# Routing both token tiles in one set of operations, and w2 in blocks of 256 columns, in a two-layer trunk with experts

## The chip, the cores and the metric

The kernel runs on one core of a Trainium2 chip. The metric is the device time of one launch in microseconds (us); each time is the median of several executions. TensorE (PE) does matmuls, VectorE (DVE), ScalarE (ACT) and GpSimd (POOL) do the elementwise work, and SyncE (SP) issues nearly all loads and stores, in one queue. The weights lie in the core's HBM in float32 and are read once each.

## The reference

A token block of 256 rows by 1024 columns passes through two layers: a state-space mixer (layer 0), then causal attention with forget gates (layer 1). Each is followed by a mixture of 32 experts, of which a token uses two. The part that the change touches is the expert mixer, and of the attention the cumulative sums of the forget gates:

```python
def hier_moe(h, wg, bg, we, be, w1, w3, w2):
    t = h.reshape(-1, d)
    g_logits = (t @ wg + bg).astype(jnp.float32)
    g_prob = jax.nn.softmax(g_logits, axis=-1)
    g_top_v, g_idx = lax.top_k(g_logits, 1)
    p_g = jnp.take_along_axis(g_prob, g_idx, axis=1)
    e_logits = (t @ we + be).astype(jnp.float32).reshape(-1, N_EXPERT_GROUPS, EXPERTS_PER_GROUP)
    e_sel = jnp.take_along_axis(e_logits, g_idx[:, :, None], axis=1)[:, 0]
    top_v, top_i = lax.top_k(e_sel, TOP_K)
    w = jax.nn.softmax(top_v, axis=-1) * p_g
    ...
    for e in range(N_EXPERTS):
        y = (jax.nn.silu(t @ w1[e]) * (t @ w3[e])) @ w2[e]
        out = out + gates[:, e:e + 1] * y.astype(jnp.float32)

# in shared_kv: forget gates, summed over the tokens
    logf = jax.nn.log_sigmoid(fz.astype(jnp.float32) + kv_fb.astype(jnp.float32))
    fcum = jnp.cumsum(logf, axis=1).transpose(0, 2, 1)

# in the trunk, for each layer: h is normalised, shifted and scaled (hn), then
        h = h + gate[:, None, :] * hier_moe(hn, moe_wg[l], moe_bg[l], moe_we[l], moe_be[l],
                                            moe_w1[l], moe_w3[l], moe_w2[l])
```

Here d = 1024, an expert's inner width is 256, there are 4 groups of 8 experts, and TOP_K is 2.

## The kernel before

The 256 tokens lie in two tiles i = 0, 1 of 128 partitions; h[:, i] is a tile's residual stream. All weights come in blocks of 1 MB (128 partitions x 2048 float32) into a ring of slots. `prefetch` and `block` (lines 69 to 84) issue a load on SP's queue as soon as a slot is free; a load waits in the queue until the instructions that read the slot before are done, and everything behind it in SP's queue waits with it. In the expert part of a layer there are 96 such blocks, in the order q = 0 to 7, for each q eight blocks "wa" (w1 and w3 of four experts) and four blocks "wb" (w2 of the same four). In layer 0 more slots are opened once the gated mixer output has been added (line 1052); in layer 1 two more groups of slots were opened in the attention part (lines 1339 and 1442).

One layer's experts, `moe` (line 312): `start` (line 571) has its order on all four compute engines written out by hand. For each tile it adds the second half of the mixer's output to h, turns the rows by four transposes (`across`), takes the sum of squares (`square`, ScalarE) and adds the logits of those columns (`logits`, line 362). Then comes the norm (`norm`, with a power on GpSimd at line 345), four steps of `fill`, which are the matmuls of the output gate (line 188, four blocks of the ring, whose row of biases is loaded by SP behind a GpSimd memset), then the routing. `route_tile` (line 365) is a generator for one tile; the two tiles' generators are run side by side with zip, so VectorE gets each operation twice in turn, 16 pairs from the logits (line 367) to the chosen experts (line 395). `weigh` ranks the tokens of each expert by small matmuls, `place` builds a selection matrix with 32 places for each expert, and `gather` (line 450) multiplies it with h, so that the tokens of four experts stand in 128 columns.

`experts` (line 595) then runs over q. `first` multiplies with the eight wa blocks (line 486): four matmuls for a block, one for each expert, on 32 columns of weights, 512 columns of the block. The activation is turned (line 474, copied at line 476 to aT), and `second` (line 495) multiplies with the wb blocks: block 2n + f holds rows 128 f to 128 f + 127 of w2 of the four experts, columns 512 n to 512 n + 511. Two blocks add up in one PSUM tile of 512 columns, which VectorE multiplies with the output gate into y (line 504). `scatter` (line 508) adds y back to the token rows: one matmul of 512 columns for each tile into four accumulators acc[i][n] that live through the layer. For the last q, `done` is called behind each of these: in layer 0 it adds the accumulator to h (line 259) and takes the sum of squares, in layer 1 it adds and issues the output DMA (line 1468). `overflow` holds a branch for experts with more than 32 tokens.

Where no order is written out, a planner with a timeline of its own orders each engine's instructions. In the attention part TensorE's order is written out, the other engines' is not (line 1145). There `project` (line 1156) runs eight steps of six matmuls (line 1162) and calls `tick` after each step. `tick` advances the first generator in the list `between` by one yield: the norm of the k heads (`head_norm`, lines 1179 to 1188), then `forget_gates` (line 1199), whose last step issues the three small matmuls of lines 1242 to 1244 on the result of a chain of small VectorE operations (lines 1220 to 1239). The accumulators of `project` come from a set of four, two for each call. The weights for each step are split in two parts by ScalarE (line 1104) and VectorE (line 1105), three steps ahead at most.

## Time and profile before

| | before |
|---|---|
| median of 3 runs | 818.82 us (817.67 to 820.29) |
| profiled execution, its own time | 819.66 us |
| its span, first to last instruction | 817.9 us |
| TensorE busy, share of the span | 706.3 us, 86% |
| VectorE busy | 381.3 us, 47% |
| ScalarE busy | 232.1 us, 28% |
| GpSimd busy | 46.7 us, 6% |
| moved by DMA | 299.30 MB, mean 366 GB/s |
| mean granted clock of TensorE | 0.945 |

A row of the timeline gives the start in us, the length in us, the engine, the line of the kernel, the operation, the tiles written and read with their shapes, and how many instructions were merged into the row; in brackets stands the idle time of the engine just before and what released it. PE is the matmul itself, PEld the load of its weights, which overlaps. A float32 matmul leaves two records. PEclk is the granted clock of TensorE as a share of 2.4 GHz.

### The profile page before, as it was taken

What the parts mean: (1) busy time and instruction counts of PE and PEld (TensorE: products, weight loads), DVE (VectorE), ACT (ScalarE), POOL (GpSimd) and SP (SyncE); (2) the same over time, 40 slices, a digit from 0 to 9 for tenths busy, and PEclk for the clock granted to TensorE, in tenths of its full rate; (3) what the DMA queues carried; (4) which work ended last, traced back from release to release, by engine and by line L of the source; (5) the groups of instructions that cost most, each with busy time, mean ns of one, the idle gap of its engine ahead of it and who ended that gap; (6) DMA issues with size and microseconds to landing.
All of it is one profiled execution on the core that took longest, in us unless ns stands there. A gap on an engine that the chain in (4) does not pass through costs nothing. (4 is left out here: it accounts for less than half of the span.)

```text
span 817.9 us, 13668 instructions
## 1 busy us (share of the span) xinstructions
PE 706.3 (86%) x5510; PEld 402.8 (49%) x5510; DVE 381.3 (47%) x1025; ACT 232.1 (28%) x537; POOL 46.7 (6%) x52
## 2 busy tenths in 40 slices
PE   2797999898899998786779899999988999986776
PEld 0674776575533533131157567888764333331311
DVE  7685999774322332111165655775554222221202
ACT  4423333162201110000043265878722101100100
POOL 2000000000000000000001101570000000000000
PEclk9899999998999999789679999999999999999888
DMA  9998946777999999999999857592989999999996
GB/s 368 426 425 347 406 150 250 292 314 277 426 426 426 426 425 425 428 423 427 424 424 426 315 197 312 204 370 98 349 347 415 426 428 424 427 427 427 425 426 260
DMA packets 41828, 299.30 MB, mean 366 GB/s; under 512 B 4632, under 2 KB 4760, under 8 KB 5664
## 3 DMA queue, kind: packets, MB, share of 16 engines
q1 hardware_dynamic: 41344, 297.14, 88.3%
q10 hardware_dynamic: 416, 1.23, 0.4%
q8 instruction: 45, 0.74, 0.3%
q14 instruction: 23, 0.19, 0.1%
HBM read 297.31 MB, written 1.05 MB: 365 GB/s over the span
## 5 line engine op out<-in xcount | busy, mean ns | idle before, releaser
L486 PE MATMUL mm<-w,xg 128*32 128x512 f32 x1024 | 141.4, 637 | 24.0 <-DMA w<-wa 10.7
L486 PEld LDWEIGHTS mm<-w,xg 128*32 128x32 f32 x1024 | 29.6, 111 | 110.6 <-issue 62.8
L458 ACT ACTIVATE xg<-mm,sh,g 128x128 f32<-128x128 f32 x64 | 29.3, 457 | 181.0 <-PE mm L450 164.8
L1105 DVE TENSOR_TENSOR ws<-w,ws 128x512 fp32r<-128x512 f32 x80 | 58.2, 733 | 40.4 <-ACT ws L1104 40.1
L501 PE MATMUL mm<-w,aT 128*32 128x512 f32 x512 | 68.3, 655 | 9.2 <-DMA w<-wb 3.6
L450 PE MATMUL mm<-Pr,h 128*128 128x128 f32 x512 | 65.3, 281 | 11.2 <-DVE Pr L438 11.2
L1162 PE MATMUL acc<-ws,hn 128*128 128x512 f32 x288 | 73.9, 415 | 0.6 <-ACT hn L1140 0.6
L450 PEld LDWEIGHTS mm<-Pr,h 128*128 128x128 f32 x512 | 60.9, 194 | 26.6 <-issue 19.0
L508 PE MATMUL acc<-y,Sc 128*128 128x512 f32 x128 | 64.7, 629 | 6.5 <-DVE y L504 6.5
L1104 ACT ACTIVATE ws<-w 128x512 fp32r<-128x512 f32 x80 | 49.9, 629 | 54.5 <-PE acc L1162 43.6
L1162 PEld LDWEIGHTS acc<-ws,hn 128*128 128x128 f32 x288 | 56.0, 197 | 16.7 <-ACT hn L1140 1.9
L456 DVE TENSOR_SCALAR xg<-mm,g,sh 128x128 f32<-128x128 f32 x64 | 26.2, 410 | 74.1 <-ACT xg L458 74.1
L504 DVE TENSOR_TENSOR y<-mm,gbc 128x512 f32<-128x512 f32 x32 | 22.1, 692 | 64.7 <-PE mm L501 64.5
L491 ACT ACTIVATE a<-mm 128x256 f32<-128x256 f32 x16 | 6.1, 383 | 161.2 <-PE mm L486 161.2
L469 DVE COPY Sc<-mm 128x256 f32<-128x256 f32 x16 | 6.8, 425 | 83.8 <-PE mm L467 83.8
L508 PEld LDWEIGHTS acc<-y,Sc 128*128 128x128 f32 x128 | 22.2, 193 | 45.6 <-issue 26.8
L492 DVE TENSOR_TENSOR a<-a,mm 128x256 f32<-128x256 f32 x16 | 6.7, 419 | 75.0 <-ACT a L491 75.0
L501 PEld LDWEIGHTS mm<-w,aT 128*32 128x32 f32 x512 | 14.4, 114 | 50.6 <-issue 34.4
L785 PE MATMUL mm<-hnT,w 128*64 128x128 f32 x512 | 33.1, 289 | 2.7 <-ACT hnT L255 2.7
L961 PE MATMUL acc<-w,uT 128*128 128x512 f32 x64 | 30.5, 621 | 5.6 <-ACT uT L950 5.5
L785 PEld LDWEIGHTS mm<-hnT,w 128*64 128x64 f32 x512 | 31.3, 143 | 4.4 <-ACT hnT L255 3.7
L173 PE MATMUL mm<-w,sc 128*32 128x256 f32 x512 | 29.2, 380 | 0.0
(327 smaller groups left out, 951.8 us busy)
## 6 DMA issues: line engine op xcount, KB each, us to landing
w<-wa SPq DMA_DIRECT2D x128, 1024.0 KB, 19.5
w<-wb SPq DMA_DIRECT2D x64, 1024.0 KB, 19.7
w<-ada SPq DMA_DIRECT2D x36, 1024.0 KB, 10.6
w<-ada00s SPq DMA_DIRECT2D x8, 1024.0 KB, 18.1
w<-kvada SPq DMA_DIRECT2D x8, 1024.0 KB, 9.0
w<-win SPq DMA_DIRECT2D x4, 1024.0 KB, 14.9
w<-ada00g SPq DMA_DIRECT2D x4, 1024.0 KB, 18.8
w<-woutv SPq DMA_DIRECT2D x4, 1024.0 KB, 17.2
```

What stands on the lines that cost most here:

```text
L173: PE.matmul(ps[32 * q:32 * q + 32, 0:256], sc32(2 * b + kk), bands(w[:, 1024 * kk:1024 * kk + 1024])[:, q], start=b + kk == 0, stop=b == 3 ...
L450: PE.matmul(px[:, 128 * c4:128 * c4 + 128], h[:, i, 128 * c:128 * c + 128], Pr[:, i].rearrange("p a b -> p (a b)"), start=i == 0, stop=i == 1)
L456: V.tensor_scalar(xg[:, c], src, g[:, c:c + 1], sh[:, c:c + 1], op0=OP.mult, op1=OP.add)
L458: S.activation(xg[:, c], src, AF.Identity, bias=sh[:, c:c + 1], scale=g[:, c:c + 1])
L486: PE.matmul(ph[32 * s:32 * s + 32, :], xg[:, k, 32 * s:32 * s + 32], w[:, 512 * s:512 * s + 512], start=k == 0, stop=k == KD - 1)
L501: PE.matmul(py[32 * s:32 * s + 32, :], aT[:, 128 * f + 32 * s:128 * f + 32 * s + 32], w[:, 512 * s:512 * s + 512], start=f == 0, stop=f == 1)
L508: PE.matmul(acc[i][n], scs[q][:, 128 * i:128 * i + 128], y[:, 512 * n:512 * n + 512], start=q == 0, stop=q == NQ - 1, skip_group_check=True)
L785: PE.matmul(ps[64 * v:64 * v + 64, 128 * hh:128 * hh + 128], w[:, k, c0:c0 + 64], hnT[:, k, v::2], start=k == 0 and hh == 0, stop=k == KD ...
L961: PE.matmul(val[t][n], uT[:, m, 128 * t:128 * t + 128], wval[m // 2][:, c0:c0 + 512], start=m == 0, stop=m == 7)
L1104: S.activation(o[:, 0], w, AF.Copy)
L1105: V.tensor_tensor(o[:, 1], w, o[:, 0].bitcast(F32), op=OP.subtract)
L1162: PE.matmul(pk[i], src[:, k, a, 128 * i:128 * i + 128], w[:, b], start=k + a + b == 0, stop=k == KD - 1 and b == 1)
```

## The change

The routing of both tiles becomes one chain: `route` works on tiles of the form [128, 2, w], both token tiles in one instruction, except for the two operations that need a scalar of each tile or more dimensions. The combination of comparing and multiplying in `rank_first` becomes two instructions, since the maximum is now broadcast. That makes 21 instructions in place of 32. In `start` the logits of the second half are issued after both tiles have been turned.

The w2 blocks are laid out anew by the host: block 2n + m now holds all 256 rows of w2 of the four experts for 256 columns, 512 n + 256 m onwards. `second` runs eight matmuls of 256 columns for a block. For the last q, `second_last` multiplies, gates, scatters and adds 256 columns at a time; the output of the last layer is stored in one DMA of 512 columns and two of 256 for each tile, six in all, where four were. In layer 0 the sum of squares is taken behind the second half. The branch in `overflow` is changed to the new layout. In `forget_gates` five empty yields stand ahead of the three small matmuls.

```diff
@@ -362,38 +362,32 @@
                 PE.matmul(pls[0][:, 64 * i:64 * i + 36], hTs[i][:, k, :], sw[:, k],
                           start=k == 0 and i == 0, stop=k == KD - 1, skip_group_check=True)
 
-        def route_tile(pl, i):
-
-            V.scalar_tensor_tensor(lg[:, i], pl[:, 64 * i:64 * i + 36], rstd[:, i:i + 1], c36, op0=OP.mult, op1=OP.add)
-            yield
-            gl = lg[:, i, 0:4]
+        def route(pl):
+
+            for i in range(2):
+                V.scalar_tensor_tensor(lg[:, i], pl[:, 64 * i:64 * i + 36], rstd[:, i:i + 1], c36,
+                                       op0=OP.mult, op1=OP.add)
 
             def rank_first(x, w, mx):
 
-                V.tensor_reduce(mx[:, i], x, axis=AX, op=OP.max)
-                yield
-                V.scalar_tensor_tensor(cand[:, i, 0:w], x, mx[:, i], desc[:, NE - w:], op0=OP.is_equal, op1=OP.mult)
-                yield
-                V.tensor_reduce(top[:, i], cand[:, i, 0:w], axis=AX, op=OP.max)
-                yield
-
-            yield from rank_first(gl, 4, gm)
-            V.tensor_scalar(gc[:, i], cand[:, i, 0:4], top[:, i], -BIG, op0=OP.is_lt, op1=OP.mult)
-            yield
-            V.tensor_tensor(ml[:, i].rearrange("p (a b) -> p a b", b=8),
-                            lg[:, i, 4:36].rearrange("p (a b) -> p a b", b=8),
-                            gc[:, i, :, None].to_broadcast([128, 4, 8]), op=OP.add)
-            yield
-            yield from rank_first(ml[:, i], NE, m1)
-            V.tensor_scalar(o1[:, i], cand[:, i], top[:, i], None, op0=OP.is_equal)
-            yield
-            V.scalar_tensor_tensor(ml2[:, i], o1[:, i], -BIG, ml[:, i], op0=OP.mult, op1=OP.add)
-            yield
-            yield from rank_first(ml2[:, i], NE, m2)
-            V.tensor_scalar(o2[:, i], cand[:, i], top[:, i], None, op0=OP.is_equal)
-            yield
-            V.tensor_tensor(selb[:, i], o1[:, i], o2[:, i], op=OP.add)
-            yield
+                V.tensor_reduce(mx[:, :, 0], x, axis=AX, op=OP.max)
+                V.tensor_tensor(cand[:, :, 0:w], x, mx.to_broadcast([128, 2, w]), op=OP.is_equal)
+                V.tensor_tensor(cand[:, :, 0:w], cand[:, :, 0:w],
+                                desc[:, None, NE - w:].to_broadcast([128, 2, w]), op=OP.mult)
+                V.tensor_reduce(top[:, :, 0], cand[:, :, 0:w], axis=AX, op=OP.max)
+
+            rank_first(lg[:, :, 0:4], 4, gm)
+            V.tensor_tensor(gc, cand[:, :, 0:4], top.to_broadcast([128, 2, 4]), op=OP.is_lt)
+            for i in range(2):
+                V.scalar_tensor_tensor(ml[:, i].rearrange("p (a b) -> p a b", b=8),
+                                       gc[:, i, :, None].to_broadcast([128, 4, 8]), -BIG,
+                                       lg[:, i, 4:36].rearrange("p (a b) -> p a b", b=8), op0=OP.mult, op1=OP.add)
+            rank_first(ml, NE, m1)
+            V.tensor_tensor(o1, cand, top.to_broadcast([128, 2, NE]), op=OP.is_equal)
+            V.scalar_tensor_tensor(ml2, o1, -BIG, ml, op0=OP.mult, op1=OP.add)
+            rank_first(ml2, NE, m2)
+            V.tensor_tensor(o2, cand, top.to_broadcast([128, 2, NE]), op=OP.is_equal)
+            V.tensor_tensor(selb, o1, o2, op=OP.add)
 
         def weigh():
 
@@ -495,20 +489,39 @@
         def second(q, aT, y, n):
 
             py = mm_tile()
-            for f in range(2):
-                w = block("wb", l, q, 2 * n + f)
-                for s in range(4):
-                    PE.matmul(py[32 * s:32 * s + 32, :], aT[:, 128 * f + 32 * s:128 * f + 32 * s + 32],
-                              w[:, 512 * s:512 * s + 512], start=f == 0, stop=f == 1)
+            for m in range(2):
+                w = block("wb", l, q, 2 * n + m)
+                for f in range(2):
+                    for s in range(4):
+                        PE.matmul(py[32 * s:32 * s + 32, 256 * m:256 * m + 256],
+                                  aT[:, 128 * f + 32 * s:128 * f + 32 * s + 32],
+                                  w[:, 512 * s + 256 * f:512 * s + 256 * f + 256],
+                                  start=f == 0, stop=f == 1, skip_group_check=True)
             c = slice(512 * n, 512 * n + 512)
             V.tensor_tensor(y[:, c], py, gbc[:, c], op=OP.mult)
 
-        def scatter(q, y, n, done=None):
+        def second_last(q, aT, y, n, done):
+
+            for m in range(2):
+                py = mm_tile()
+                w = block("wb", l, q, 2 * n + m)
+                for f in range(2):
+                    for s in range(4):
+                        PE.matmul(py[32 * s:32 * s + 32, 0:256],
+                                  aT[:, 128 * f + 32 * s:128 * f + 32 * s + 32],
+                                  w[:, 512 * s + 256 * f:512 * s + 256 * f + 256], start=f == 0, stop=f == 1)
+                c = slice(512 * n + 256 * m, 512 * n + 256 * m + 256)
+                V.tensor_tensor(y[:, c], py[:, 0:256], gbc[:, c], op=OP.mult)
+                for i in range(2):
+                    PE.matmul(acc[i][n][:, 256 * m:256 * m + 256], scs[q][:, 128 * i:128 * i + 128], y[:, c],
+                              start=False, stop=True, skip_group_check=True)
+                    V.tensor_tensor(h[:, i, c], acc[i][n][:, 256 * m:256 * m + 256], h[:, i, c], op=OP.add)
+                    done(i, n, m)
+
+        def scatter(q, y, n):
             for i in range(2):
                 PE.matmul(acc[i][n], scs[q][:, 128 * i:128 * i + 128], y[:, 512 * n:512 * n + 512],
-                          start=q == 0, stop=q == NQ - 1, skip_group_check=True)
-                if done:
-                    done(i, n, acc[i][n])
+                          start=q == 0, stop=False, skip_group_check=True)
 
         def overflow(rv):
 
@@ -556,10 +569,12 @@
                     for n in range(2):
                         w = part("wb", n)
                         py = [mm_tile() for _ in range(2)]
-                        for f in range(2):
-                            for i in range(2):
-                                PE.matmul(py[i], aTs[i][:, 128 * f:128 * f + 128], w[:, f],
-                                          start=f == 0, stop=f == 1)
+                        for m in range(2):
+                            for f in range(2):
+                                for i in range(2):
+                                    PE.matmul(py[i][:, 256 * m:256 * m + 256], aTs[i][:, 128 * f:128 * f + 128],
+                                              w[:, m, 256 * f:256 * f + 256], start=f == 0, stop=f == 1,
+                                              skip_group_check=True)
                         for i in range(2):
                             for c2 in range(2):
                                 r = slice(256 * c2, 256 * c2 + 256)
@@ -578,13 +593,13 @@
                     next(st)
                     across(i, 1)
                     square(ssq, i, 1)
+                for i in range(2):
                     logits(i, 1)
                 after()
                 mb.append(es.enter_context(tc.tile_pool(name=f"moeb{l}", bufs=1, side="right")))
                 norm(ssq)
                 step(fill, 4)
-                for _ in zip(*[route_tile(pls[0], i) for i in range(2)]):
-                    pass
+                route(pls[0])
                 mosti = weigh()
                 place(0)
                 gather(0)
@@ -612,13 +627,12 @@
                     gather(q + 1)
                 aT = turned(a)
                 y = mb[0].tile([128, D], F32, tag="y", name="y", bufs=2)
-                second(q, aT, y, 0)
                 if last:
-                    scatter(q, y, 0, done)
-                second(q, aT, y, 1)
-                if last:
-                    scatter(q, y, 1, done)
+                    second_last(q, aT, y, 0, done)
+                    second_last(q, aT, y, 1, done)
                 else:
+                    second(q, aT, y, 0)
+                    second(q, aT, y, 1)
                     scatter(q, y, 0)
             if l == 0:
                 shrink()
@@ -1055,9 +1069,9 @@
 
     ssq2 = new_ssq()
 
-    def add_square(i, n, src):
-        add(src, i, n)
-        square(ssq2, i, n)
+    def add_square(i, n, m):
+        if m:
+            square(ssq2, i, n)
 
     gb11 = gate_tile(small)
     M.experts(mosti, fill, add_square)
@@ -1238,6 +1252,8 @@
         V.tensor_scalar(fz, fz, 0.0, None, op0=OP.min)
         V.scalar_tensor_tensor(fz, fp, -2.0, fz, op0=OP.mult, op1=OP.add)
         yield
+        for _ in range(5):
+            yield
         pc = mm_tile()
         PE.matmul(pc[:, 0:16], tri, fz[:, 0:16], start=True, stop=True)
         PE.matmul(pc[:, 16:32], ones, fz[:, 0:16], start=True, stop=False)
@@ -1462,10 +1478,10 @@
 
     mosti = M.start(added, ssq, fill, lambda: None)
 
-    def add_out(i, n, src):
-        add(src, i, n)
-        c = slice(512 * n, 512 * n + 512)
-        nc.sync.dma_start(out[0, 128 * i:128 * i + 128, c], h[:, i, c])
+    def add_out(i, n, m):
+        if n or m:
+            c = slice(512 + 256 * m, 768 + 256 * m) if n else slice(0, 512)
+            nc.sync.dma_start(out[0, 128 * i:128 * i + 128, c], h[:, i, c])
 
     M.experts(mosti, fill, add_out)
     er.close()
@@ -1561,7 +1577,7 @@
 
     w13 = np.concatenate([np.asarray(moe_w1), np.asarray(moe_w3)], axis=-1)
     d["wa"] = w13.reshape(2, NQ, 4, KD, 128, 512).transpose(0, 1, 3, 4, 2, 5).reshape(2, NQ, KD, 128, 2048)
-    d["wb"] = (np.asarray(moe_w2).reshape(2, NQ, 4, 2, 128, 2, 512).transpose(0, 1, 5, 3, 4, 2, 6)
+    d["wb"] = (np.asarray(moe_w2).reshape(2, NQ, 4, 2, 128, 4, 256).transpose(0, 1, 5, 4, 2, 3, 6)
                .reshape(2, NQ, 4, 128, 2048))
     return {n: np.ascontiguousarray(a) for n, a in d.items()}
```

## Rows read from the trace of the kernel before

**Rows 1.** Windows: start:end, length, busy us (instructions) by engine, PEclk, DMA share, GB/s.

```profile
200.00:400.00 200.00, 168.50 (x1121) 66.17 (x1113) 47.43 (x150) 20.48 (x45) 0.22 (x2) 0.93 1.01 425
565.00:570.00 5.00, 4.63 (x28) 3.40 (x28) 2.32 (x4) 5.00 (x11) 0.00 (x0) 1.00 0.01 3
...
603.50:606.50 3.00, 3.00 (x32) 1.46 (x34) 2.08 (x17) 0.00 (x0) 1.17 (x2) 1.00 0.01 4
607.00:807.00 200.00, 167.17 (x1117) 65.64 (x1110) 46.76 (x145) 20.48 (x45) 0.00 (x0) 0.94 1.01 424
```

**Rows 2.** Waits of TensorE, 461 to 604 us: releaser, us in total, times, longest.

```profile
PE mm L1242 <- DVE f_z L1239: 3.9, 1, 3.9
PE mm L188 <- DVE xf L1136: 0.9, 1, 0.9
```

**Rows 3.** Windows behind the wait at line 1242, columns as in rows 1.

```profile
462.00:465.00 3.00, 3.00 (x9) 2.32 (x8) 0.17 (x3) 0.63 (x1) 0.00 (x0) 0.50 1.02 430
466.00:470.00 4.00, 4.00 (x19) 3.22 (x18) 1.65 (x3) 1.90 (x3) 0.00 (x0) 1.00 0.02 10
```

**Rows 4.** Timeline of the attention part: head norm of k, and eight steps.

```profile
450.32 0.60 ACT L1179 ACTIVATE sq<-acc 128x512 f32<-128x512 f32 x1 [0.53 <-PE acc L1162]
...
455.92 0.69 DVE L1188 TENSOR_TENSOR kn<-acc,rs 128x512 f32<-128x512 f32 x1
...
489.25 11.45 PE L1162 MATMUL acc<-ws,hn 128*128 128x512 f32 x48
```

**Rows 5.** Timeline of the tail of layer 0.

```profile
403.00 3.78 PE L508 MATMUL acc<-y,Sc 128*128 128x512 f32 x4 [0.80 <-DVE y L504]
...
409.75 1.98 PE L508 MATMUL acc<-y,Sc 128*128 128x512 f32 x4 [0.83 <-DVE y L504]
...
411.77 0.69 DVE L259 TENSOR_TENSOR h<-acc,h 128x512 f32<-128x512 f32 x1 [0.17 <-PE acc L508]
```

**Rows 6.** Timeline: matmuls of 256 and 512 columns, and copies of aT.

```profile
433.20 3.66 PE L173 MATMUL mm<-w,sc 128*32 128x256 f32 x64
...
627.11 0.42 DVE L476 COPY aT<-mm 128x256 f32<-128x256 f32 x1 [0.49 <-PE mm L474]
...
630.13 3.64 PE L501 MATMUL mm<-w,aT 128*32 128x512 f32 x32
...
649.25 0.42 DVE L476 COPY aT<-mm 128x256 f32<-128x256 f32 x1 [0.49 <-PE mm L474]
...
802.97 0.42 DVE L476 COPY aT<-mm 128x256 f32<-128x256 f32 x1 [0.78 <-PE mm L474]
```

**Rows 7.** Timeline of the start of the experts of layer 1.

```profile
596.85 0.60 PE L333 MATMUL mm<-ident,h 128*128 128x128 f32 x4
...
599.21 2.84 PE L362 MATMUL acc<-smallw,hT 128*128 128x36 f32 x24
...
604.31 3.64 PE L188 MATMUL acc<-w,sc 128*32 128x512 f32 x32
...
604.50 0.42 DVE L367 SCALAR_TENSOR_TENSOR lg<-acc,rstds,c 128x36 f32<-128x36 f32 x2 [0.92 <-POOL rstds L345]
...
608.33 0.32 DVE L395 TENSOR_TENSOR selb<-o,o 128x32 bf16<-128x32 f32 x2
...
614.12 7.07 PE L486 MATMUL mm<-w,xg 128*32 128x512 f32 x64
```

**Rows 8.** Timeline of small VectorE operations of 32 and 64 elements.

```profile
459.07 1.32 DVE L1236 SCALAR_TENSOR_TENSOR f_p<-f_p,f 128x32 f32<-128x32 f32 x6
...
608.96 0.23 DVE L410 SCALAR_TENSOR_TENSOR rk<-mm,selb 128x64 f32<-128x64 f32 x1 [0.17 <-PE mm L409]
```

**Rows 9.** Timeline of the tail of layer 1.

```profile
811.06 0.69 DVE L504 TENSOR_TENSOR y<-mm,gbc 128x512 f32<-128x512 f32 x1 [0.34 <-PE mm L501]
...
811.80 1.98 PE L508 MATMUL acc<-y,Sc 128*128 128x512 f32 x4 [0.81 <-DVE y L504]
```

**Rows 10.** Output stores: from the issue to landing, by tile.

```profile
DMA to landing us min/median/max: 2.0/2.0/2.0
```

## The prediction

> **What bounds the kernel now.** First read the load queue over time. From 200 to 400 us, while the experts of layer 0 run, and from 607 to 807 us, while those of layer 1 run, the 16 DMA engines are busy 1.01 of the time at some 425 GB/s [rows 1]. Nothing on the engines can shorten these 400 us; they can only begin or end at another time. Between them lies the attention part, where the DMA engines have free time: between 565 and 570 us they move nearly nothing [rows 1]. There TensorE is the bound. Its list of waits from 461 to 604 us holds one that matters, 3.9 us before line 1242, then 0.9 us [rows 2]. So time can be won at four places: in the tail of layer 0 (from its last blocks to the rows' sums of squares), at line 1242, at the point where the loads of layer 1 start again after a gap (603.5 to 606.5 us, DMA share 0.01 [rows 1]), and in the tail of layer 1, which ends the kernel. What is won ahead of the gap is worth its full length only if the loads ahead of the gap can move forward too; the idle 565 to 570 us say that they wait for free slots there, and slots come free when TensorE and ScalarE have read them.
>
> **Line 1242 (five more yields).** TensorE's order is written out in this part. After two steps of the first v projection it meets the three small products of the forget gates and waits 3.9 us for VectorE's chain of small operations [rows 2]. The wait has a second price: from 462 to 465 us the granted clock is 0.50, that is 1.2 GHz, after TensorE had stood idle, and from 466 us it is 1.00 [rows 3]. 3 us at half speed lose 1.5 us. The new yields let five more steps go first. Eight steps take 11.45 us [rows 4], so five take 7.2 us, against 3.9 us of wait. VectorE must put the splits of weights that feed these steps between the chain; two or three of 0.7 us delay the chain by about 2 us, to some 6 of the 7.2 us. The wait then goes to nothing, and no idle is left to lower the clock: 3.9 + 1.5 = **5.4 us**. The bounds are 3.9 (no gain from the clock) and 5.6 us (half speed until nearly 466). Behind the moved products waits only the first turning of heads, 40 us later. What is moved with them is the head norm of the second half of k, now generated five ticks later; it frees two of the four accumulators that the second v projection wants. In the trace its last multiplication already runs at 455.92 us [rows 4], ten us before that projection, so I cost this at nothing; without that cover it is the first rival.
>
> **Tail of layer 0.** TensorE has idle gaps of 0.80 and 0.83 us where it waits for the gate product of 512 columns on VectorE, and after the second it still has 1.98 us of scatter, then the add of 0.69 us [rows 5]. With blocks by 256 columns a half of y is ready after each block. The first gap closes, for the first half's scatter can begin while the second block is multiplied. In place of the second gap stands the scatter of the half before (half of 1.98). After the last gate product only two matmuls of 256 columns and one add of 256 columns are left. So the last scatter ends 0.80 + 0.83 = 1.63 us earlier and the last add is some 0.27 us shorter (512 columns take 0.69; a 256 column copy from PSUM, line 476, takes 0.42 [rows 6]): **1.9 us**. The work of TensorE stays the same, since 64 records of 128x256 took 3.66 us and 32 of 128x512 took 3.64 us [rows 6]. The low bound is 0.8 us (only one gap closes); the high one is 3.2, if the first scatter, 3.78 us here against 1.98 later [rows 5], runs partly at the higher clock because TensorE has stood idle less before it. Behind this tail TensorE waits for sums of squares and the norm, so the gain passes on whole.
>
> **Start of the experts.** In layer 0 the new order and the new routing change nothing: the loads run at a share of 1.01 throughout [rows 1], and the slack of the ring absorbs either sign. In layer 1 the loads stand still until the ada11 blocks of line 188 are read (from 604.31 us), and a second time they nearly run dry until the first block of line 486 is read (from 614.12 us) [rows 7]. The turned rows of tile 1 now go ahead of all logits of the start. Line 362 takes 2.84 us for 24 records, from 599.21 [rows 7]; with four transposes of 0.6 us ahead of it [rows 7] and eight more records (1.0 us) it ends at 599.2 + 0.6 + 2.84 + 1.0 = 603.65, so line 188 starts 0.66 us earlier and line 367, which then no longer waits for the norm, at 603.75 in place of 604.50 us, 0.75 earlier. Against this stands the routing itself. Now 32 small operations in 16 pairs take 3.83 us from line 367 to line 395 [rows 7], 0.26 a pair: the two tiles' operations overlap, so a pair costs about what one dependent operation costs. After the change there are 21 operations in 19 dependent steps, 18 of them ahead of the last. A dependent step of 32 elements takes 1.32/6 = 0.22 us; 64 elements add about 0.035 (0.225 against 0.19 for one operation) [rows 8]. 0.26 for the logits' pair, 6 x 0.22, 11 x 0.255 make 4.4 us, 0.6 more than now. Line 486 starts 0.75 - 0.6 = **0.15 us** earlier, and this second point decides. Bounds: a loss of 0.7 us (18 steps of 0.30, a pair of now and 64 elements, make 5.3) and a gain of 1.0 (routing much shorter, line 188 deciding). The Trainium skill speaks here for a larger gain (VectorE: DVE Perf Modes, Rules for kernel authors): it tells one to lower the count of chained VectorE operations, since each waits for the pipeline to empty. By that, 21 in place of 32 would take 2.5 us, not 4.4; the trace speaks against it, since independent neighbours here start some 0.13 us apart, closer than their own lengths.
>
> **Tail of layer 1.** The chain is gate product 0.69, during which and a little beyond TensorE waits 0.81, scatter 1.98 [rows 9], add 0.69 [rows 5], then an output DMA of 2.0 us to landing [rows 10]. The first scatter already hides behind the blocks, so one gap closes (0.8 us) and the add shrinks by 0.27: **1.05 us**. Six output DMAs take the place of four on SP; no load is queued behind them. Low bound 0.5 (the scheduler puts the half's scatter ahead of the last block, so that part of the wait stays), high 1.4 (the last DMA carries half the bytes).
>
> **The sum.** 5.4 + 1.9 + 0.15 + 1.05 = 8.5 us. The profiled execution took 819.66 us (span 817.9), so 811.2; it lies 0.84 above the median 818.82, and the median becomes **810.3 us**. With all low bounds the gain is 4.5 (814.3), with all high ones 11.2 (807.6). The loop over the other seven q of a layer keeps its time: it moves the same bytes.
>
> **Rivals.** (a) The stall only changes its place: the second v projection waits for the accumulators that the late head norm still reads. That chain took from 450.3 to 456.6 us [rows 4]; begun only at the products' new turn it would cost about what the wait costs now, and the gain is 3.1 us: 815.7. Against it: VectorE's and ScalarE's orders are not written out here, and they run the norm as soon as its sums are there. (b) The loads ahead of the gap don't move forward, so that only the idle 3.0 us of 603.5 to 606.5 can be won there, and 1.05 in the tail: 814.8. Against it: the idle time at 565 us. (c) Slower: a matmul of 256 columns costs nearly what one of 512 costs. Then the four w2 blocks of a q take 3.64 us more. One q takes 649.25 - 627.11 = 22.14 us on TensorE while the ring is full; 627.11 + 7 x 25.78 = 807.6 is then 4.6 us past the last copy of aT at 802.97 [rows 6], and the tail's four blocks add 3.6: 8.2 us in each layer, 16.4 - 8.5 = 7.9 slower, 826.7. It turns to a loss once a 256 column matmul costs 0.93 of the larger one: 8 x growth - 20.9 = 4.25 in each layer gives 3.14 us of growth in a q. Against it: line 173, with the same 32 column weights, at 3.66 us for 64 [rows 6]. The Trainium skill speaks for it in kind (TensorE: Matmul & The Clock Gate, Back-to-back issue gap): in a stream, weight load and matmul together set the spacing, so that short matmuls come out dearer than their columns; line 173 shows none of it at 256. (d) The routing goes by count of operations, and line 188 decides: some 0.5 us more gain, 809.8.
>
> **How the numbers follow.** Forecast 0.68; (a) 0.11; (b) 0.05; (d) 0.04; (a) and (b) in one with tails that don't pay, 0.06, which is no measurable change; (c) or a like loss 0.06. A measurement of this kernel tells 0.3%, 2.5 us, from none. Faster: 0.68 + 0.11 + 0.05 + 0.04 = 0.88; same 0.06; slower 0.06. The forecast's bounds with (b) and (d) hold 0.77; reaching to (a) gives 0.88: 807.6 to 815.7.
>
> **What the profile will show.** Right: no wait worth naming before the products of the forget gates, granted clock 1.00 in the steps behind them, and everything from there to the gap some 7 us earlier; line 188 and the first block of the experts of layer 1 earlier against line 259 by 0.7 and 0.1 to 0.2 us; the routing from its first operation to selb some 4.4 us; the last scatter directly behind TensorE's last block with only a half in it. Wrong: a TensorE wait for an accumulator at the start of the second v projection; loads that run without a gap from 573 us on; w2 groups of 256 columns that take more than 0.95 us a block at the higher clock; or the same distance from the last w2 block to the last add as now.

## The result, and the profile after

The changed kernel takes 810.49 us (median of 6 runs, 807.84 to 811.36) against 819.30 us for the kernel before in the same comparison: ratio 0.9898, 95% interval 0.9882 to 0.9914. That is 8.8 us, where 8.5 were forecast. The profiled run took 810.06 us, with a span of 808.2 us. The total came out as worked out; three of its four terms did not, and the sections below take them apart.

Both kernels were profiled a second time in the last comparison. The table cuts each span at the same instructions, by their start and end times in the timeline; the last two columns are what was won between first and first, and second and second profile.

| stretch (us) | before 1 | before 2 | after 1 | after 2 | won 1 | won 2 |
|---|---|---|---|---|---|---|
| start of the program to the last block of line 486 (480 after) in layer 0 | 395.45 | 395.31 | 394.62 | 393.94 | 0.83 | 1.37 |
| from there to the end of the last add of layer 0 | 17.01 | 14.88 | 13.68 | 13.68 | 3.33 | 1.20 |
| to the first k projection (line 1162, 1176 after) | 7.20 | 7.20 | 8.25 | 8.25 | -1.05 | -1.05 |
| to the first of the last two adds of line 259 ahead of layer 1's experts | 178.06 | 177.69 | 172.11 | 170.53 | 5.95 | 7.16 |
| to the first block of the experts of layer 1 | 16.40 | 17.34 | 17.74 | 17.73 | -1.34 | -0.39 |
| to the last block of line 486 (480) in layer 1 | 185.48 | 185.33 | 185.26 | 185.55 | 0.22 | -0.22 |
| to the end of the last add | 14.92 | 14.95 | 13.55 | 14.75 | 1.37 | 0.20 |
| to the end of the span | 3.37 | 3.38 | 2.99 | 3.00 | 0.38 | 0.38 |

Two profiles of one kernel differ by up to 2.1 us in a stretch whose code is the same. That is the first thing to see: a term of 1 to 2 us can't be read from one profile alone.

Windows of the kernel after, columns as in rows 1 (which they answer):

```profile
200.00:400.00 200.00, 165.61 (x1342) 73.55 (x1338) 45.79 (x136) 20.51 (x45) 0.22 (x2) 0.94 1.01 425
555.00:560.00 5.00, 4.26 (x23) 2.83 (x22) 2.53 (x5) 5.00 (x12) 0.00 (x0) 1.00 0.00 0
600.00:800.00 200.00, 167.35 (x1360) 77.19 (x1360) 46.26 (x132) 20.10 (x43) 0.00 (x0) 0.94 1.00 419
460.00:464.00 4.00, 4.00 (x22) 3.33 (x22) 1.83 (x5) 2.04 (x4) 0.00 (x0) 1.00 1.01 427
```

The load-bound stretch of layer 0 is what it was. The window in layer 1 starts ahead of the experts' first block and holds a short standstill of the loads (606 to 610 us: DMA share 0.50), hence 419 GB/s in place of 424. The idle time of the load queue that stood at 565 to 570 us [rows 1] stands at 555 to 560 now, so the loads ahead of the gap moved forward with TensorE. The stretch behind the forget gates has a granted clock of 1.00, where it was 0.50 [rows 3].

TensorE's waits of the kernel after, 400 to 604 us, columns as in rows 2, the longest four:

```profile
PE mm L1143 <- DMA w<-wk: 4.4, 1, 4.4
PE mm L399 <- DVE selb L390: 1.4, 1, 1.4
PE mm L444 <- DVE Pr L432: 1.2, 1, 1.2
PE mm L188 <- DVE xf L1150: 0.9, 1, 0.9
```

No wait stands before the products of the forget gates any more (3.9 us before [rows 2]), and none for accumulators at the second v projection. Timeline of the kernel after around the products:

```profile
450.62 10.06 PE L1176 MATMUL acc<-ws,hn 128*128 128x512 f32 x42
...
459.42 0.19 DVE L1253 SCALAR_TENSOR_TENSOR f_z<-f_p,f_z 128x32 f32<-128x32 f32 x1
...
460.52 0.29 PE L1258 MATMUL mm<-f_z,tri 128*128 128x16 f32 x2
```

VectorE's chain ends at 459.61 us, 0.9 us before TensorE comes to the products. Timeline of the kernel after, tail of layer 0 up to the first projection (rows 5 answer to its first lines):

```profile
404.49 1.07 PE L510 MATMUL mm<-w,aT 128*32 128x256 f32 x16 [0.30 <-DMA w<-wb]
...
405.49 2.35 PE L516 MATMUL acc<-y,Sc 128*128 128x256 f32 x8
...
407.44 0.86 DVE L518 TENSOR_TENSOR h<-acc,h 128x256 f32<-128x256 f32 x2 [0.36 <-PE acc L516]
407.87 1.15 ACT L1118 ACTIVATE ws<-w 128x512 fp32r<-128x512 f32 x2 [3.23 <-PE acc L516]
...
408.93 0.58 ACT L226 ACTIVATE mm<-h 128x512 f32<-128x512 f32 x1
...
411.32 0.75 DVE L234 TENSOR_SCALAR xs<-h,rstd 128x1024 f32<-128x1024 f32 x1 [0.44 <-POOL rstd L233]
...
412.28 3.65 PE L1143 MATMUL mm<-ident,xs 128*128 128x128 f32 x16 [4.44 <-DMA w<-wk]
...
416.55 0.80 PE L1176 MATMUL acc<-ws,hn 128*128 128x512 f32 x1 [0.62 <-ACT hn L1154]
```

The first add of the last pair is done at 407.87 us, but ScalarE first runs two splits of weights (line 1118, 1.15 us) and only then the square of that tile (line 226, 408.93). The wait of 4.4 us before line 1143 is put down to a load of wk, but these transposes read xs, which VectorE finishes at 412.07 us: TensorE waits for the chain of square, norm and xs. Timeline of the kernel after, start of the experts of layer 1 (rows 7):

```profile
594.39 0.42 DVE L368 SCALAR_TENSOR_TENSOR lg<-acc,rstds,c 128x36 f32<-128x36 f32 x2 [1.65 <-PE acc L362]
...
596.68 0.23 DVE L375 TENSOR_TENSOR cand<-cand,desc 128x64 f32<-128x64 f32 x1
596.95 0.22 DVE L377 TENSOR_REDUCE top<-cand 128x2 f32<-128x64 f32 x1
...
599.00 0.23 DVE L390 TENSOR_TENSOR selb<-o,o 128x64 bf16<-128x64 f32 x1
...
599.29 0.19 PE L399 MATMUL mm<-selb,trib 128*128 128x32 bf16 x1 [1.44 <-DVE selb L390]
...
600.79 5.67 PE L444 MATMUL mm<-Pr,h 128*128 128x128 f32 x32 [1.22 <-DVE Pr L432]
...
606.40 1.06 PE L480 MATMUL mm<-w,xg 128*32 128x512 f32 x8
```

The routing takes 599.00 - 594.39 = 4.61 us from its first operation to selb (3.83 before [rows 7]); operations of 64 elements start 0.26 to 0.27 us apart. The gather's 32 records of matmuls take 5.67 us; in the first profile of before the same 32 (line 450, from 610.14) took 4.04. From 602 to 605 us, inside them, the granted clock is 0.51. The chain of the kernel after that ended last (start, us, what):

```profile
799.07 1.07 PE mm L510 x16
800.14 1.93 PE acc L516 x8
802.07 1.04 PE mm L510 x16
803.11 0.02 issue
803.13 0.44 DVE y L514
803.57 0.04 issue
803.61 0.71 PE acc L516 x2
804.33 0.02 issue
804.35 0.42 DVE h L518
```

Timeline of the same place:

```profile
802.00 1.07 PE L510 MATMUL mm<-w,aT 128*32 128x256 f32 x16
...
803.61 1.13 PE L516 MATMUL acc<-y,Sc 128*128 128x256 f32 x4 [0.55 <-DVE y L514]
```

Behind the last block stand one gate product of 256 columns and that half's scatter, as forecast. But the scatter of the half before stands ahead of the block (800.14), not behind it, so that 0.55 us of wait are left; rows 9 had 0.69, 0.81 of wait and 1.98. And 64 records of matmuls of 256 columns in the loop over q:

```profile
622.42 3.66 PE L496 MATMUL mm<-w,aT 128*32 128x256 f32 x64
```

### The profile page after: what moved, and what is told of

It is laid out like the page before. It is cut to its first block, busy times and chain, and to the rows that moved or that the text cites. A ratio compares the mean times of both kernels' runs of the same rounds, so it can differ in the third digit from the quotient of the medians.

```text
span 808.2 us, 14723 instructions
## 1 busy us (share of the span) xinstructions
PE 698.6 (86%) x6038; PEld 422.1 (52%) x6038; DVE 381.5 (47%) x1015; ACT 232.0 (29%) x537; POOL 46.7 (6%) x52
## 3 DMA queue, kind: packets, MB, share of 16 engines
HBM read 297.31 MB, written 1.05 MB: 369 GB/s over the span
## 5 line engine op out<-in xcount | busy, mean ns | idle before, releaser
L480 PE MATMUL mm<-w,xg 128*32 128x512 f32 x1024 | 133.4, 622 | 28.7 <-DMA w<-wa 19.5
L444 PE MATMUL mm<-Pr,h 128*128 128x128 f32 x512 | 67.2, 288 | 11.3 <-DVE Pr L432 11.2
L444 PEld LDWEIGHTS mm<-Pr,h 128*128 128x128 f32 x512 | 62.8, 200 | 24.2 <-issue 17.2
L1176 PE MATMUL acc<-ws,hn 128*128 128x512 f32 x288 | 72.1, 407 | 0.6 <-ACT hn L1154 0.6
L496 PE MATMUL mm<-w,aT 128*32 128x256 f32 x896 | 61.5, 416 | 9.5 <-DMA w<-wb 5.0
L523 PE MATMUL acc<-y,Sc 128*128 128x512 f32 x112 | 57.0, 633 | 3.3 <-DVE y L501 3.3
L496 PEld LDWEIGHTS mm<-w,aT 128*32 128x32 f32 x896 | 29.3, 116 | 39.3 <-issue 19.6
L501 DVE TENSOR_TENSOR y<-mm,gbc 128x512 f32<-128x512 f32 x28 | 19.4, 692 | 63.8 <-PE mm L496 63.5
L523 PEld LDWEIGHTS acc<-y,Sc 128*128 128x128 f32 x112 | 19.9, 198 | 32.2 <-issue 20.7
```

Of the source, the lines that this page charges most:

```text
L444: PE.matmul(px[:, 128 * c4:128 * c4 + 128], h[:, i, 128 * c:128 * c + 128], Pr[:, i].rearrange("p a b -> p (a b)"), start=i == 0, stop=i == 1)
L480: PE.matmul(ph[32 * s:32 * s + 32, :], xg[:, k, 32 * s:32 * s + 32], w[:, 512 * s:512 * s + 512], start=k == 0, stop=k == KD - 1)
L496: PE.matmul(py[32 * s:32 * s + 32, 256 * m:256 * m + 256], aT[:, 128 * f + 32 * s:128 * f + 32 * s + 32], w[:, 512 * s + 256 * f:512 * s + ...
L523: PE.matmul(acc[i][n], scs[q][:, 128 * i:128 * i + 128], y[:, 512 * n:512 * n + 512], start=q == 0, stop=False, skip_group_check=True)
L1176: PE.matmul(pk[i], src[:, k, a, 128 * i:128 * i + 128], w[:, b], start=k + a + b == 0, stop=k == KD - 1 and b == 1)
```

## The experiments

My theory behind the forecast was that the gain is made of the yields (5.4), the two tails (1.9 and 1.05) and a start of the experts that gains nothing to speak of (0.15). The first profile seemed to say that the start costs 1.3 us, and that the clock at its gather is to blame; the rival was that half clock turns up by itself. First the parts alone.

**The yields alone** (the kernel before with this edit):

```diff
         yield
+        for _ in range(5):
+            yield
         pc = mm_tile()
```

> The kernel before with the five yields alone. Theory from the two traces: between the first matmul of the k projection (419.66 and 416.55 us) and the first add of layer 1 (597.72 and 588.66 us) the changed kernel wins 5.95 us, of which 3.89 us are the wait at the forget gates and about 1.7 us the half clock behind it; so 5.4 to 6.0 us faster than before, about 0.993 of it. Rival: only the wait goes, the clock falls for another reason: 3.9 us, 0.995. Rival (a) of the prediction, the stall moves to the accumulators: 0 to 1 us.

Measured: 813.13 us, ratio 0.9927 (0.9902 to 0.9951), 6.0 us faster. The stretch from the first k projection to the adds is 172.05 us long (178.06 before). The yields carry most of the gain, as worked out. The interval reaches from 4.0 to 8.0 us, though, so timing alone doesn't say whether the clock behind the wait is in it.

**The blocks of w2 and the last sums alone** (second, second_last, add_square, add_out and the layout of wb as in the changed kernel):

```diff
-            for f in range(2):
-                w = block("wb", l, q, 2 * n + f)
+            for m in range(2):
+                w = block("wb", l, q, 2 * n + m)
+                for f in range(2):
...
-                second(q, aT, y, 0)
...
+                    second_last(q, aT, y, 0, done)
+                    second_last(q, aT, y, 1, done)
```

> The kernel before with the w2 blocks by 256 columns and the last sums in steps of 256 columns alone. Theory from the two traces: the tail of layer 0 gives 2.3 us, that of layer 1 1.3 us to the last add and 0.4 us behind it, so 4.0 us in all, 0.995 of before. The prediction's own numbers: 1.9 + 1.05 = 2.95 us, 0.9964. Rival (c), dearer matmuls: slower than before.

Measured: 815.61 us, ratio 0.9959 (0.9942 to 0.9977), 3.4 us faster, where the prediction's terms gave 2.95. With the 3.66 us above against 3.64 for the same columns in 32 [rows 6] there is no loss in the loop, and rival (c) falls. That 3.4 comes near 2.95 is weaker than it looks. In this profile the tail of layer 0 with the way to the first projection takes 14.53 + 8.18 = 22.71 us, against 24.21 and 22.08 in the two profiles of before; the tail of layer 1 to the end of the span takes 17.29, against 18.3 in both. Against the second profile the tails win 0.4 us of a span that is 3.6 us shorter (812.5 against 816.1), against the first 2.5 of 5.4. The rest lies outside the tails, and what the 3.4 us are made of is not shown. The rule of the Trainium skill that was weighed for it (TensorE: Matmul & The Clock Gate, Back-to-back issue gap) shows nothing here at 256 columns.

**The order of the start and the new routing, and the order alone** (both from the kernel before; the second without the routing):

```diff
                     square(ssq, i, 1)
+                for i in range(2):
                     logits(i, 1)
...
-                for _ in zip(*[route_tile(pls[0], i) for i in range(2)]):
-                    pass
+                route(pls[0])
```

> The kernel before with the new order of the start and the new routing alone. Theory from the two traces: in layer 1 the first block of the experts comes 1.3 us later against the first add, and the loads stand still the second time for about 2.2 in place of 0.5 us; layer 0 hides everything; so 1.1 to 1.4 us slower than before, 1.0015. The prediction's step: 0.15 us faster, 0.9998. Rival (d): 0.7 us faster.

> The kernel before with the new order of the start alone (both tiles turned ahead of the logits), the routing as before. Theory: line 188 and the routing start 0.7 to 1.0 us earlier, the wait between them and the clock stay as they are, so the first block of the experts and the end come 0.7 to 1.0 us earlier, 0.999. Rival: the loads bind elsewhere and nothing comes of it, 1.000.

Measured: with both 818.17 us, ratio 0.9981 (0.9967 to 0.9994), 1.6 us faster by that ratio; with the order alone 817.62 us, ratio 0.9978 (0.9964 to 0.9992), 1.8 us faster. So the start doesn't make the kernel slower, and the loss read from one profile was a miss. The 0.2 us between the two lie within either interval: timing can't show here what the routing costs. Parts don't quite add up either: 6.0 + 3.4 + 1.6 = 11.0 against 8.8, within the intervals.

**The old routing in the changed kernel:**

```diff
-                route(pls[0])
+                for _ in zip(*[route_tile(pls[0], i) for i in range(2)]):
+                    pass
```

> The changed kernel with the routing of before (32 operations in pairs), all else as changed. Theory: the new routing takes 4.61 us from its first operation to selb where the old one takes 3.83 (traces of both), and the second standstill of the loads in layer 1 passes this on; so 0.6 to 0.8 us faster than the changed kernel, 0.989 of before. Rival (d) and the Trainium skill's rule on the count of operations: slower than the changed kernel by about 0.7 us, 0.9907.

Measured: 809.43 us, ratio 0.9877 (0.9857 to 0.9897). The interval overlaps with that of the changed kernel (0.9882 to 0.9914), so timing doesn't tell the two apart. In the trace the routing takes 3.83 us again, and the start 16.98 us in place of 17.74, 0.76 shorter; the gather still takes 5.67.

**One more matmul behind the gate matmuls** (128x512 into scratch, work that the reference doesn't need), so that TensorE stands idle less before line 399:

```diff
                 step(fill, 4)
+                PE.matmul(mm_tile(), ident, h[:, 0, 0:512], start=True, stop=True)
                 route(pls[0])
```

> The changed kernel with one matmul of 128x512 into a scratch tile behind the matmuls of the output gate (line 188), where TensorE stands idle 1.44 us for the routing. In the trace of the changed kernel the gather behind it ran at a granted clock of 0.50 and took 5.67 us in place of 4.04. Theory 1: the idle time lowered the clock; then the gather takes 4.0 us again and the end comes 1.3 us earlier, 0.988 of before. Theory 2: the stretch of half clock falls now here, now there in each kernel (in e1, with the start and routing of before, it fell on the gate matmuls); then nothing changes in the median, 0.990, and the profile shows half clock somewhere near or not at all.

Measured: 808.53 us, ratio 0.9876 (0.9861 to 0.9892). Timeline of this kernel:

```profile
597.66 1.12 PE L602 MATMUL mm<-h,ident 128*128 128x512 f32 x2
599.16 0.19 PE L399 MATMUL mm<-selb,trib 128*128 128x32 bf16 x1 [0.37 <-DVE selb L390]
...
600.66 5.67 PE L444 MATMUL mm<-Pr,h 128*128 128x128 f32 x32 [1.22 <-DVE Pr L432]
```

The idle time before line 399 went from 1.44 to 0.37 us, and the gather is as slow as before. That this idle time causes it is not borne out. The wait of 1.22 us right ahead of the gather, for Pr, is still there.

**The wait at the forget gates filled with matmuls** (the kernel before with four scratch matmuls in the place of the wait):

```diff
         yield
+        for _ in range(4):
+            PE.matmul(mm_tile(), ident, h[:, 0, 0:512], start=True, stop=True)
         pc = mm_tile()
```

> The kernel before, where the wait of 3.9 us ahead of the products of the forget gates is filled with four matmuls of 128x512 into scratch tiles, 3.4 us of work in all. The wait for VectorE stays. Theory: what the yields win is the wait and, apart from it, the half clock behind it; here only the second goes, 1.5 to 1.7 us faster than before, 0.998, and the granted clock behind the products is 1.00. Rival: the idle time does not set the clock; no change, or 0.2 us slower.

Measured: 819.18 us, ratio 1.0003 (0.9989 to 1.0016): nothing, a miss in the total. TensorE's waits of this kernel, 455 to 612 us, and its timeline at the start of layer 1's experts:

```profile
PE mm L1244 <- DVE f_z L1239: 0.5, 1, 0.5
```

```profile
600.93 6.05 PE L188 MATMUL acc<-w,sc 128*32 128x512 f32 x32
```

The mechanism did what it should: the wait is 0.5 us, the granted clock behind it 1.00 (459 to 463 us), and the stretch to the adds is 176.42 us, 1.6 less than in the first profile of before. But in this run the gate matmuls of line 188 took 6.05 us, not 3.64 [rows 7], at a granted clock of 0.52 (602 to 606 us), and from add to first block it is 18.90 us. In this profile the clock given back at one place was lost at another; whether the medians are equal for that reason is argued, not shown.

**Old routing, and one more matmul on each w1 block of the last q** (scratch work), to keep the clock up in both tails:

```diff
                 if k in between:
+                if q == NQ - 1:
+                    PE.matmul(mm_tile(), xg[:, k, :], w[:, 0:512], start=True, stop=True)
+                if k in between:
                     between[k]()
```

> e5 with one more matmul (128 columns of weights, 512 columns) into a scratch tile on each wa block of the last q, where TensorE waits for loads 1.4 of every 2.45 us. Theory: TensorE enters the two tails at the higher clock, the last wa block takes 1.07 in place of 1.55 to 1.9 us and the activation's turning and the first w2 blocks likewise; 0.5 to 1.0 us for each tail against e5, 0.987 of before. Rival: the added work holds the clock no better, and each block's own matmuls come up to 0.9 us later; 0 to 1 us slower than e5.

Measured: 809.09 us, ratio 0.9884 (0.9869 to 0.9899), no better than with the old routing alone. The granted clock is 1.00 from 395 to 409 and from 791 to 806 us, and yet the tails take 14.95 and 14.47 us, against 13.74 and 14.81 with the old routing alone. But the planner's order differs as well: each half's scatter now stands right behind its block and waits 0.54 to 1.03 us for the gate product, four times in layer 0. So this run doesn't show what the clock alone is worth in the tails.

**Both kernels once more**, for a second profile:

> The changed kernel once more, unchanged, beside the two that follow. The total: ratio to before 0.989 to 0.991 again (8 to 9 us faster). In its trace, theory 1 (the stretches at half clock sit at places that the order of the work fixes): from the first add of the last pair of adds ahead of the experts of layer 1 to their first block 17.7 us again, with the gather's 32 matmuls in 5.67 us at a granted clock of 0.50. Theory 2 (they fall by chance from run to run): the gather near 4.04 us and the start near 16.1 us in this profile.

> The kernel before once more, unchanged, for a second profile. Theory 1 (half clock sits at fixed places): the first scatter of layer 0's tail takes 3.78 us for 4 matmuls again, last block to last add 17.0 us again, and the start of the experts of layer 1 16.4 us with the gate matmuls at 3.64 us. Theory 2 (the tail in the first profile was an odd case): the tail takes 14.6 to 15.0 us, as in all variants that keep its code, the first scatter some 2.0 us, and the half clock may turn up elsewhere, at the gate matmuls (4.8 to 6.1 us in place of 3.64).

Measured: the changed kernel 809.61 us, ratio 0.9885 (0.9866 to 0.9905), the kernel before 817.88 us in its one profiled run. Timeline of the second profile of before:

```profile
402.37 1.98 PE L508 MATMUL acc<-y,Sc 128*128 128x512 f32 x4 [0.82 <-DVE y L504]
...
601.67 5.34 PE L188 MATMUL acc<-w,sc 128*32 128x512 f32 x32
...
608.45 4.04 PE L450 MATMUL mm<-Pr,h 128*128 128x128 f32 x32 [1.22 <-DVE Pr L438]
```

The first scatter of the tail takes 1.98 us here, not 3.78 [rows 5], and the gate matmuls 5.34, not 3.64 [rows 7]. In the five other profiles with the old tail's code in layer 0 (the second of before, the yields, the start with and without the routing, the filled wait) it takes 14.6 to 15.0 us; 17.0 was the odd one. The first profile of the changed kernel and then its second, windows (columns as in rows 1) over the first 4 us of the k projections:

```profile
416.50:420.50 4.00, 3.96 (x9) 3.11 (x10) 2.71 (x5) 2.63 (x5) 0.00 (x0) 0.50 1.01 426
```

```profile
415.90:419.90 4.00, 4.00 (x16) 2.97 (x17) 3.73 (x7) 3.63 (x7) 0.00 (x0) 1.00 1.01 426
```

Half clock in the one, full clock in the other, by the same code, the same 4.4 us of wait ahead of it and the same 3.65 us of transposes. The gather was at half clock both times (5.67 us). So neither "fixed places" nor "chance" holds throughout: some places repeat, some don't.

**The squares first** (the changed kernel; three writes of one column make the first splits wait for the last sums of squares):

```diff
     ready, rest, rest_blocks = [], [], []
+    first_ws = [1, 1, 1]
...
         o = tp.tile([128, 2, 512], F32R, tag="ws", name="ws", bufs=3)
+        if first_ws:
+            S.activation(o[:, 0, 0:1], ssq2[:, 1, 1:2], AF.Copy)
+            first_ws.pop()
         S.activation(o[:, 0], w, AF.Copy)
```

> The changed kernel, where the first three splits of weights behind layer 0's tail wait for the last sums of squares (one column of them is first written into each split's tile, three activations of 128x1 more). Theory 1 (the new tail ends its adds about 1 us earlier than the old one, but gives it back, since ScalarE now runs two splits, 1.15 us, ahead of the squares): from the last add of layer 0 to the first projection 6.6 to 7.2 us in place of 8.2, and the total 1.0 to 1.6 us under the changed kernel, ratio some 0.988. Rival (the first projection waits for something else, the splits themselves or the transposes): the distance stays near 8.2, and the total with it.

Measured: 808.25 us, ratio 0.9858 (0.9833 to 0.9882), 1.4 us under the changed kernel beside it, though their runs overlap a little (806.09 to 808.99 against 808.67 to 810.86). Timeline:

```profile
407.56 0.58 ACT L226 ACTIVATE mm<-h 128x512 f32<-128x512 f32 x1
...
408.59 1.65 ACT L1122 ACTIVATE ws<-w 128x512 fp32r<-128x512 f32 x3
...
409.57 3.65 PE L1147 MATMUL mm<-ident,xs 128*128 128x128 f32 x16 [2.77 <-DMA w<-wk]
...
413.83 2.50 PE L1180 MATMUL acc<-ws,hn 128*128 128x512 f32 x5 [0.61 <-ACT hn L1158]
```

The last add ends at 407.27 us, so the way to the first projection is 6.57 us, against 8.25: the splits ahead of the squares were what took the tail's gain. It is also less than the 7.20 of before, where three splits stood between the last two squares. In this profile the first projections were at half clock again (414 to 418 us: 0.50), so that its span, 807.1 us, hardly differs from 807.4 in the second profile of the changed kernel; the gain shows in the medians.

**Three edits in one:** squares first, old routing, and the scratch matmul behind the gate matmuls (work that the reference doesn't need).

> The changed kernel with the squares first, the old routing on each tile by itself, and one more matmul of 128x512 into scratch behind the gate matmuls (work that the reference doesn't need). Theory 1 (new routing costs 0.78 us, squares 1.0 to 1.6 us): 1.8 to 2.4 us under the changed kernel, ratio some 0.987. Rival (what is won ahead of the loads is lost to a longer stretch at half clock at the start of the experts): within 0.5 us of the kernel with the squares first alone.

Measured: 806.56 us (805.90 to 806.87), ratio 0.9847 (0.9830 to 0.9865), 3.05 us under the changed kernel beside it, whose fastest run took 808.67. It beats both kernels. Timeline at the start of layer 1's experts:

```profile
596.41 4.05 PE L450 MATMUL mm<-Pr,h 128*128 128x128 f32 x32 [1.22 <-DVE Pr L438]
600.39 1.06 PE L486 MATMUL mm<-w,xg 128*32 128x512 f32 x8
```

Here the gather runs at full clock, and the start takes 600.39 - 584.84 = 15.55 us. With one profile it stays open whether old routing and filled gap together bring that about, or this run merely had it so. And little of it reaches the end: from the first to the last block of layer 1 it is 187.22 us here, against 185.25 to 185.55 in the profiles of the changed kernel and with the old routing, the filled gap or the squares first alone. The span is 3.3 us shorter than in the second profile of the changed kernel: 1.7 us of that stand between the tail of layer 0 and the first projection, 0.5 between the adds and the last block of layer 1, and 1.2 in the last tail, where that profile had a stretch at half clock (794 to 798 us: 0.57).

## Why the prediction was right, point by point

**The yields** (5.4 forecast): 6.0 by timing. In the traces the stretch is 5.95 and 7.16 us shorter, but half clock at its beginning differs. From windows of 1 us, the clock is 0.50 for 4.8 and 3.9 us behind the first projection in the two profiles of before, for 4.1 us in the first of after, for none in the second. Taking half of each off leaves 175.7 twice against 170.1 and 170.5: 5.2 to 5.6 us. Wait and clock behind it both went, and the loads moved with them. The clock's part repeats: in all five profiles with the wait of 3.9 us (both of before, the blocks alone, the start with and without the routing) the granted clock falls to 0.50 there for 3 to 7 us; in the nine without it, the filled wait among them, it stays at 1.00 from 440 to 480 us. Rivals (a) and (b) fall.

**Tail of layer 0** (1.9): the step failed in three places. The base was a slow scatter of 3.78 us [rows 5] in a profile with 17.0 us for the tail; to the last add 3.33 us were won against that profile, 1.20 against the second. Of the two gaps, closing the first won nothing against the second profile: from the last block of line 486 (480) to the last w2 block it is 9.86 us in the second profile of before and 9.87 in both of the changed kernel, where TensorE, though earlier, waits for that block's load (404.49, 0.30 us). What is won lies behind that block. And "the gain passes on whole" was wrong: ScalarE's queue was not looked at. It had two splits ahead of the last two squares, so 1.05 us went back, and 0.15 us is left against the second profile. The run with the squares first shows it.

**Start of the experts** (0.15): the two parts came out with the right signs and near sizes. From the first of the last two adds to the first operation on the logits it is 594.39 - 588.66 = 5.73 us against 604.50 - 597.72 = 6.78 before, 1.05 earlier (0.75 forecast); the routing is 0.78 us longer (0.6 forecast: steps of 64 elements came at 0.26 as counted and those of 8 at 0.20 in place of 0.22, but the two pairs that still go tile by tile, the logits and their masking, took 0.46 and 0.33, not 0.26 and 0.22). Left over, 0.27 us would be won. What the step lacked is the clock: the gather took 1.63 us more. Against the first profile of before, which had full clock all through the start, that makes a loss of 1.34; against the second, with 5.34 us for the gate matmuls, 0.39. The step also took the first block for the point that decides, and that held in part only: from the first of the last two adds to the last block of layer 1 it is 201.9 and 202.7 us before, 203.0 and 203.3 in the changed kernel, 202.2 with the old routing, and 202.8 with three edits in one, where the first block came 2.2 us earlier than in the changed kernel. Rival (d), the routing by count of operations, falls: 21 operations took longer than 32, since a dependent step costs 0.26 us whether one operation of 64 elements or a pair of 32 stands in it. The rule of the Trainium skill (VectorE: DVE Perf Modes, Rules for kernel authors) fits the length of one chain here, not the count of operations in two that run side by side.

**Tail of layer 1** (1.05): the size is near, the make-up is not the forecast's. From the last w2 block to the end of the last add it is 4.60 and 4.59 us in the two profiles of before and 3.21 in both of the changed kernel, 1.4 us less. The prediction counted 0.8 for the wait and 0.27 for the add. The add gave its 0.27; but the scheduler put the scatter of the half before ahead of the last block, the case of the low bound, so the wait gave only 0.26 (0.55 in place of 0.81), and 0.85 came from the last scatter (1.13 in place of 1.98), which the sum had not counted. Over the whole tail 1.37 us were won to the last add in the first profile of after and 0.20 in the second, where the clock fell to 0.57 from 794 to 798 us, ahead of that block; 0.38 us more lie behind the last add in both. The sum, 0.6 to 1.8 us, has the forecast in its middle and a little of it above the high bound of 1.4. What makes the 0.38 us isn't shown: the smaller stores take 2.1 us to landing, the old ones 2.0 [rows 10].

**What the sum left out:** 0.8 and 1.4 us that are won by the first add ahead of layer 0's experts (179.24 and 179.19 us before, 178.49 and 177.75 after), in code ahead of all edits. There the same 64 records of matmuls of layer 0 (line 948, 962 after) took 3.61 and 3.44 us in the two profiles of before, 3.41 and 1.95 in those of after; in the first pair 0.58 us was already there when that line started. A forecast can't hold that; it is the spread of one run.

So the total was right because its largest term was right and well founded, and because the errors in the small ones, 1.05 us given back in layer 0, 0.6 to 1.1 us lost from the adds to the last block of layer 1, some 1 us won upstream, are of both signs. That they leave 0.2 us between 810.49 and the forecast 810.3 is luck.

## What to carry to other kernels

Where a wait in a hand-written order is followed by a stretch at half clock, moving independent work into it paid wait and clock here; filling it with idle work paid nothing in the total. Follow a gain in a tail through the queue of every engine behind it up to the next matmul: an engine that came free earlier had taken other work first, and one added dependence won 1.7 us in its stretch (1.4 between the medians). For terms under 2 us, profile both kernels twice and compare only stretches at the same granted clock.

## What the runs showed of the hardware

The granted clock falls to half at several places of this kernel, mostly in or just after a wait of TensorE: 3.9 us at the forget gates, 4.4 ahead of the k projections, 2.2 ahead of line 957. But it also fell at the gate matmuls of the second profile of before, after a wait of 0.8 us, and in the gather of the filled gap, after waits of 0.37 and 1.22 us. And apart from the forget gates, where it came with the wait in all five profiles, whether and for how long it falls differs from run to run of the same program. Timeline of line 962 in layer 0 in the first and the second profile of the changed kernel:

```profile
157.51 3.41 PE L962 MATMUL mm<-m,cz 128*32 128x128 f32 x64
```

```profile
158.20 1.95 PE L962 MATMUL mm<-m,cz 128*32 128x128 f32 x64
```

Ahead of both TensorE waited 2.2 us before line 957. The kernels with the squares first and with three edits in one ran side by side on one chip and have the same code up to here; they took 1.95 and 3.47 us, so it isn't a matter of the chip. One such stretch costs 1.4 to 2.4 us, as much as the smaller edits of this change bring. What decides is left open.
